# One encoder layer on one core: smaller first loads, wider attention products and a changed order of some loads

## The chip, the core and the metric

The kernel runs on one core of a Trainium2 chip. The core has a matrix engine (TensorE, PE in the profile; its weight loads are listed apart as PEld), three engines for element-wise work (VectorE or DVE, ScalarE or ACT, GpSimd or POOL), and a synchronisation engine (SyncE, SP) whose queue issues most of the transfers between HBM and the on-chip memory. Matrix products write to eight banks of an accumulator memory (PSUM). The metric is the time of one execution on the device, in microseconds (us); lower is better.

## What is computed

One layer of an encoder for two sequences of 512 tokens, width 1024, in float32: a state-space branch, a differential attention branch and a cross attention to 256 memory rows, gated and merged, then a feed-forward block. Cut to what the change touches:

```
def _diff_attention(q, k, v, lam, subln_g, lambda_init):
        s = jnp.einsum('bqhd,bkhd->bhqk', qblk, k).astype(jnp.float32) * scale
        probs = jax.nn.softmax(s, axis=-1).reshape(Bn, DIFF_HEADS, 2, Q_BLOCK, L)
        w = probs[:, :, 0] - lam * probs[:, :, 1]
        return jnp.einsum('bhqk,bkhe->bqhe', w.astype(v.dtype), v)
...
    mk, mv = jnp.split(mn @ p['w_mem_kv'][l], 2, axis=-1)
    y_x = _cross_attention(xq.reshape(Bn, L, X_HEADS, X_DH), mk, mv)
    for n in range(N_BRANCH):
        term = jax.nn.sigmoid(g[..., n * D_MODEL:(n + 1) * D_MODEL]) * (branches[n] @ p['w_up'][l, n])
        merged = term if merged is None else merged + term
    x = x + merged @ p['w_out'][l]
    xn2 = _rmsnorm(x, p['norm_ffn'][l])
    gate, up = jnp.split(xn2 @ p['w_ffn_in'][l], 2, axis=-1)
    return x + (jax.nn.silu(gate) * up) @ p['w_ffn_out'][l]
```

## The kernel before

**Products.** Every float32 operand is split into a high and a low half (`split`, L131: a copy on ScalarE that rounds, a subtraction on VectorE that keeps the rest), and each product is made as three: high by high, high by low, low by high. One product instruction takes 128 rows of weights and up to 512 columns.

**Order.** The program is written in one order, and a planner places each engine's instructions by a simulated timeline; an engine then runs its own list strictly in order. `tc.issue_after(x)` holds the instructions of its block behind `x` on the engine of `x` alone. `queued()` (L293) is such a block behind `last_w`, the last weight load so far, and so concerns SP's list. From L687 on (and again from L1166), `PE.on` keeps TensorE's list in the written order.

**The start (L304 to L322).** TensorE first multiplies zeros, `NWARM` times (L305). The loop at L311 then loads the first weight of the memory projection in two halves of 256 KB, each followed by `mem_part(i)` (L222), which loads two of the eight rows of the transposed memory in one transfer of 512 KB and splits them, scaled by a column of `vec`. `vec` itself is loaded at L118, first in SP's list. `mem_part(2)` and `mem_part(3)` follow. `mem_k(0, ...)` makes three products for each of the eight rows, in the order of the rows; `mem_k(1, ...)` follows with the second weight.

**Differential attention (L829 to L938).** There are 32 steps, one for each head `h`, sequence `s` and block `qt` of 128 queries. `scores(i)` makes the scores of two steps and their softmax; `turn(i)` transposes the 128 by 512 weights of a step on TensorE and splits them into `pH` and `pL` (tag `pT`, 4 slots); `outputs(i)` multiplies them by the values, after each second step, with 256 queries at a time; `squares` and `normed` finish a head three steps on. Between them `fill(n)` puts products from `queue`: projections, and at its end `merges()`, which multiplies branch outputs by `w_up` (`merge_units`: 24 products each). Branch outputs are loaded by `merge_load` and split by `merge_split`; `merge_in(2)` (L816) does both for the four tiles of branch 2 at one place, ahead of the third unit.

**Feed-forward, first half (L1153 to L1198).** 22 rounds of 84 products. Each round makes four sums of weights on POOL (L1040 to L1043), scales two results there (`up`, L1182) and, in rounds 4 to 18, prepares a part of the weights of the second half (`half_piece`, L1198): 128 by 128 sums on POOL (`raw_sums`, L454 to L457), a split, and a store to `wD`.

**Feed-forward, second half (L1215 to L1338).** 36 pieces of 21 products, in twelve visits (`VISITS`, of 2, 3, 3, 4, ... pieces). A piece needs two weight tiles, `wD` loads at L1255 (384 KB) and L1253 (512 KB) for the first 16 pieces; six rooms hold the weights of three pieces, so a piece's loads start when the piece three before it is done. Activations come in pairs: `pair_in` (L1211) loads two tiles of 512 KB (`fa`, `fb`, L1139 and L1140), makes sums of them and splits seven quarters. A visit starts from `y`, loaded at L1293. The last tile of activations is stored at L1318.

Of the kernel before, what the change touches and what calls it, by code (L numbers as in the profile page):

```python
# [19 lines left out]
P = 128  # L20
L = 512
# [19 lines left out]

NG = (7, 6, 3)

NWARM = 13

SCAN = (33, 40, 47, 53, 60)
ROUND = 12582912.0
# [25 lines left out]
def encoder(ctx: ExitStack, tc: tile.TileContext, a, out):  # L73
# [41 lines left out]

    ident = cst.tile([P, P], F32, name="ident")
    vec = cst.tile([P, N_VEC], F32, name="vec")
    nc.sync.dma_start(vec, a["vecs"])  # L118
# [7 lines left out]
    def vcol(name, i=0):  # L126
        o = VEC[name][0] + i
        return vec[:, o : o + 1]
# [92 lines left out]

    def mem_part(i):  # L222
        mt_ = slot("ld", [P, 2, L], name="mt")
        nc.sync.dma_start(mt_, a["memT"][:, 2 * i : 2 * i + 2, :])
        for j in range(2):
            split(mh[i][:, j, :], ml[i][:, j, :], mt_[:, j, :], scale=vcol("norm_mem", 2 * i + j))

    last_sq = None
# [79 lines left out]

    wf = wp.tile([P, DM], F32, tag="wf", name="wf")
    wh, wl = (wp.tile([P, DM], F32R, tag=n_, name=n_) for n_ in ("wh", "wl"))  # L310
    for i in range(2):  # L311
        hs = slice(i * L, (i + 1) * L)
        nc.sync.dma_start(wf[:, hs], a["w_mk"][0][:, hs])
        split(wh[:, hs], wl[:, hs], wf[:, hs])
        mem_part(i)
    mw = [(wh, wl)]
    mem_part(2)
    mem_part(3)
    mw.append(weight(a["w_mk"][1]))
    with queued():  # L320
# [412 lines left out]
    phase.close()  # L733


    open_tags(phase, v2=2, qk=12, pT=4)
    aes = ExitStack()
    ap_ = aes.enter_context(tc.tile_pool(name="att", bufs=2, reuse_waits="tile"))
    acol = aes.enter_context(tc.tile_pool(name="acol", bufs=2, reuse_waits="tile"))
# [38 lines left out]
        split(h_, l_, yt, scale=(0.125, None, 0.5)[n])  # L778
        b[0][t], b[1][t] = h_, l_

    def merge_in(n, tags="yyyy"):
        b = [None] * 4, [None] * 4
        for t in range(4):
            merge_split(b, n, t, tags[t], merge_load(n, t))
        return b

    def merge_units(n, b, m, first=False, last=False):
        gt = slot("ld", name="gl")
        nc.sync.dma_start(gt, gD[n * KD + m])
# [14 lines left out]
            split(mgh[m], mgl[m], mg[m])  # L804

    mes, zes = ExitStack(), ExitStack()
    b0, b1 = (([None] * 4, [None] * 4) for _ in range(2))
    b1_in = []

    def merges():  # L810
        res_.close()
        xp_es.close()
        open_tags(mes, side="right", mg=8, y=8)
        for m in range(KD):
            if m == 2:
                b2 = merge_in(2)  # L816
            yield from merge_units(0, b0, m, first=True)
        for m in range(KD):
            yield from merge_units(2, b2, m)
# [43 lines left out]

    def turn(i):
        h, s, qt = steps[i]
        if qt % 2 == 0:
            pT[h, s, qt // 2] = tuple(slot("pT", [P, 4, 2 * P], F32R, n_) for n_ in ("pH", "pL"))
        e0 = es.pop(i)
        tr = aux()
        for j in range(4):  # L870
            PE.transpose(tr[:, j * P : (j + 1) * P], e0[:, j * P : (j + 1) * P], ident)
        ps = slice(qt % 2 * P, qt % 2 * P + P)
        split(*(p_[:, :, ps] for p_ in pT[h, s, qt // 2]), tr.rearrange("p (j q) -> p j q", j=4))

    def outputs(i):

        h, s, qt = steps[i]
        if h == 2 and s == qt - 1 == 0:
# [11 lines left out]
        if qt == 3:  # L890
            o_ = rp.tile([P, L], F32, tag="nsq", name="osb", bufs=2)
            S.copy(o_, osb[h, s])
            osb[h, s] = o_

    def squares(i):
        h, s, _ = steps[i]
# [18 lines left out]
    for i in range(-1, n + 3):  # L915
        if i % 2 and i + 1 < n:
            scores(i + 1)
        fill(10 if i < n - 1 else 16)
        if 0 <= i < n:
            turn(i)  # L920
        if 0 < i <= n and steps[i - 1][2] % 2:
            outputs(i - 1)
        fill(10)
        if 1 < i <= n + 1 and steps[i - 2][2] == 3:
            squares(i - 2)
        if i > 2 and steps[i - 3][2] == 3:
            normed(i - 3)
        if i in (17, 19, 21, 23):
            t = (0, 1, 3, 2)[(i - 17) // 2]
            with yielding(last_e):  # L930
                merge_split(b0, 0, t, "v" if t == 3 else "qk", first[t])
        if i in (15, 17, 19, 21):
            t = (0, 1, 3, 2)[(i - 15) // 2]
            first[t] = merge_load(0, t)
# [214 lines left out]
                pass  # L1149
        return w  # L1150

    nxt_w, last_t = res0, None
    for i in range(KFF):  # L1153
        w = nxt_w or all7(i)
        nxt_w = None
        if i == 4:
            prep = prepare(pes, pieces[NPREP[0] : NPREP[1]])
            next(prep)
        elif i == KFF - 3:
            assert next(prep, None) is None  # L1160
            pes.close()
            open_tags(fes, side="right", tsa=1, tsb=1)
        if i == KFF - 1:
            with tc.issue_after(last_s[1].ins):
# [12 lines left out]
        def activate(s, gf, up):  # L1177
            nonlocal last_t
# [3 lines left out]
            PO.tensor_tensor(out=up, in0=up, in1=accs[s], op=ALU.mult)  # L1182
            V.scalar_tensor_tensor(out=ac[:, cs], in0=ac[:, cs], scalar=1.0, in1=gf, op0=ALU.add, op1=ALU.mult)
            V.tensor_tensor(out=ac[:, cs], in0=ac[:, cs], in1=up, op=ALU.mult)

        if i == KFF - 1:
            with tc.issue_after(last_sum.ins):
                activate(0, gf0, up0)
            break
        with ExitStack() as es_:  # L1190
            if i == KFF - 2:
                nxt_w = all7(i + 1)
                es_.enter_context(tc.issue_after(last_s[1].ins))
            activate(0, gf0, up0)
# [82 lines left out]
    for v, (m, lo_, hi_) in enumerate(VISITS):  # L1277
        ps = [bank() for _ in range(6)] + [aux()]
        for p in range(lo_, hi_):
            if n_p + 3 < len(pieces) and not pieces[n_p + 3][2]:  # L1280
                next(coming[n_p + 3])
            if n_p + 2 < len(pieces):
                next(coming[n_p + 2])
            for g in coming[n_p + 1 : n_p + 2]:
                for _ in g:
                    pass
            th, tl = pairs[p]
            w = made[n_p]
            n_p += 1
            if v < 4 and p == 1:  # L1290
                with queued():
                    for t in (m, m + 4):
                        nc.sync.dma_start(y[t], x1D[t])  # L1293
            for p_, (nm, o) in zip(ps, SEVEN):
                wh, wl = w[nm]
                PE.matmul(p_, wh, th[:, o], start=(p == lo_), stop=False)
                PE.matmul(p_, wh, tl[:, o], start=False, stop=False)
                PE.matmul(p_, wl, th[:, o], start=False, stop=(p == hi_ - 1))
            if v == 3 and p == 0:
                with tc.issue_after(last_sum.ins):  # L1300
                    pair_in()
            if (v, p) in ((10, 7), (10, 8), (11, 7), (11, 8)):
                keep(2)
# [11 lines left out]
            with queued(), tc.issue_after(last_sum.ins):  # L1315
                pair_in()
        if v == 2:
            nc.sync.dma_start(aD[KFF - 1], ac)  # L1318
# [520 lines left out]
```

## Time and profile before

| What | us |
|---|---|
| median of 3 runs | 1592.64 (1591.06 to 1593.86) |
| profiled execution, whole | 1595.11 |
| profiled execution, span | 1593.3 |
| PE busy in the span | 1577.1 (99%) |
| DVE, ACT, POOL busy | 1162.6, 631.0, 532.9 |
| mean granted TensorE clock | 0.996 |

The span is the time from the first to the last instruction of the program; 1.8 us of the profiled execution lie around it. The profiled execution is 2.5 us longer than the median of the runs. A row of the timeline gives the start, the duration, the engine, the line, the operation with the tiles it writes and reads, the number of merged instructions, and in brackets the idle time before it and what ended it. Products overlap, so a product's duration (0.39 us) is longer than the distance to the next one. In the view by windows each engine has its busy time and its count of instructions, followed by the granted clock (PEclk), the share of the 16 transfer engines that was busy, and GB/s.

### The profile page before, as it was taken

Reading aid. Unit: us, or ns where it says so; the run is one execution under the profiler, and the core shown is the slowest. Engines: PE = TensorE matmul, PEld = TensorE weight load, DVE = VectorE, ACT = ScalarE, POOL = GpSimd, SP = SyncE. Lnnn points to the kernel's source line nnn. Section 1 sums busy time; section 2 is a strip of 40 time slices with the busy share of each in tenths; the row PEclk is TensorE's granted clock in tenths of the full one; section 3 lists DMA queues with packets and bytes.
Section 4 is the critical chain, followed back from the end, with each engine's and each line's share of the span. In section 5 each row is a group of like instructions: output and inputs, shape, how many; then the busy total and the mean of one; then the engine's idle time right before and its main releaser. Section 6 shows DMA issues by size and latency. Waiting matters only on the chain.

```text
span 1593.3 us, 21527 instructions
## 1 busy us (share of the span) xinstructions
PE 1577.1 (99%) x7838; PEld 1317.1 (83%) x7838; DVE 1162.6 (73%) x1858; ACT 631.0 (40%) x1114; POOL 532.9 (33%) x434
## 2 busy tenths in 40 slices
PE   9999999999999999999999999999999999999997
PEld 7888888888898789878888888888888888788787
DVE  7978995077773776865545578888888878978864
ACT  6644223275652465563223343233332333223323
POOL 0010000001333320300443355766676543444663
PEclk9999999999999999999999999999999999999998
DMA  9554623576762121154543522333333323985312
GB/s 363 178 167 127 205 93 124 177 265 209 255 225 102 52 89 41 47 162 149 192 145 119 146 85 94 108 104 120 119 129 124 111 93 116 331 320 190 125 60 106
DMA packets 104890, 237.84 MB, mean 149 GB/s; under 512 B 13520, under 2 KB 45008, under 8 KB 104784
## 3 DMA queue, kind: packets, MB, share of 16 engines
q1 hardware_dynamic: 104784, 236.47, 44.0%
q8 instruction: 61, 1.00, 0.3%
q14 instruction: 45, 0.37, 0.1%
HBM read 165.16 MB, written 71.27 MB: 148 GB/s over the span
## 4 chain that ended last, share of the span: by engine, by line
PE 90%; DVE 3%; POOL 3%; DMA 2%; issue 1%; SPq 0%; ACT 0%; POOLq 0%; DVEq 0%; ACTq 0%
PE bkmm L66 78%; PE bktr L66 4%; PE bkoo L66 2%; PE bktr L69 2%; PE bksc L66 1%; PE bktr L1673 1%; DMA w<-wD 1%; DVE wl L135 1%; PE bktr L1642 1%; DMA aD<-ac 1%; PE bktr L1734 0%; PE bktr L1733 0%; PE bktr L1732 0%; PE bktr L1609 0%; DMA mt<-in_memT 0%
## 5 line engine op out<-in xcount | busy, mean ns | idle before, releaser
L66 PE MATMUL bkmm<-xh,wh 128*128 128x512 f32 x640 | 254.4, 398 | 0.0
L66 PE MATMUL bkmm<-xh,wl 128*128 128x512 f32 x640 | 250.5, 392 | 0.0
L66 PE MATMUL bkmm<-xl,wh 128*128 128x512 f32 x640 | 250.1, 391 | 0.0
L66 PE MATMUL bkmm<-th,wl 128*128 128x512 f32 (+1 forms) x621 | 240.9, 388 | 0.6 <-DVE wl L135 0.6
L66 PE MATMUL bkmm<-tl,wh 128*128 128x512 f32 (+1 forms) x621 | 241.1, 388 | 0.0
L66 PE MATMUL bkmm<-th,wh 128*128 128x512 f32 (+1 forms) x621 | 240.7, 388 | 0.0
L134 ACT CAST wh<-wf 128x1024 fp32r<-128x1024 f32 (+1 forms) x133 | 117.4, 883 | 245.2 <-PE bkmm L66 178.5
L135 DVE TENSOR_TENSOR wl<-wf,wh 128x1024 fp32r<-128x1024 f32 (+1 forms) x133 | 149.9, 1127 | 61.3 <-ACT wh L134 56.9
L66 PE MATMUL bkmm<-th,w 128*128 128x512 f32 x432 | 142.1, 395 | 3.4 <-DMA w<-wD 2.7
L66 PEld LDWEIGHTS bkmm<-xh,wh 128*128 128x128 f32 x640 | 120.3, 188 | 26.2 <-issue 3.4
L66 PEld LDWEIGHTS bkmm<-xh,wl 128*128 128x128 f32 x640 | 120.2, 188 | 26.1 <-issue 0.4
L66 PEld LDWEIGHTS bkmm<-xl,wh 128*128 128x128 f32 x640 | 120.4, 188 | 22.2
L66 PEld LDWEIGHTS bkmm<-th,wl 128*128 128x128 f32 x621 | 116.5, 188 | 25.0 <-DVE wl L135 1.1
L66 PEld LDWEIGHTS bkmm<-tl,wh 128*128 128x128 f32 x621 | 116.6, 188 | 24.0
L66 PEld LDWEIGHTS bkmm<-th,wh 128*128 128x128 f32 x621 | 116.6, 188 | 23.8
L454 POOL TENSOR_TENSOR raw<-raw 128x128 f32<-128x128 f32 x28 | 15.9, 572 | 312.4 <-DVE nb L545 230.2
L1182 POOL TENSOR_TENSOR up<-up,acc 128x512 f32<-128x512 f32 x44 | 82.4, 1891 | 80.1 <-DVE up L1120 76.4
L66 PEld LDWEIGHTS bkmm<-th,w 128*128 128x128 f32 x432 | 81.7, 189 | 24.3 <-DMA w<-wD 3.4
L800 POOL TENSOR_TENSOR mg<-mg,gl 128x1024 f32<-128x1024 f32 x16 | 43.8, 2739 | 138.3 <-DVE gl L796 133.7
L66 PE MATMUL bkmm<-tl,w 128*128 128x512 f32 x216 | 84.7, 392 | 0.0
L66 PE MATMUL bkmm<-yh,wh 128*128 128x512 f32 x192 | 76.1, 396 | 0.0
L1181 ACT ACTIVATE ac<-gf 128x512 f32<-128x512 f32 x44 | 27.8, 633 | 119.5 <-DVE gf L1180 61.0
(661 smaller groups left out, 3563.6 us busy)
## 6 DMA issues: line engine op xcount, KB each, us to landing
wf<-in_w_in SPq DMA_DIRECT2D x40, 512.0 KB, 4.0
wD<-hl SPq DMA_DIRECT2D x28, 512.0 KB, 2.9
w<-wD SPq DMA_DIRECT2D x28, 512.0 KB, 4.7
gD<-gt SPq DMA_DIRECT2D x24, 512.0 KB, 3.0
gl<-gD SPq DMA_DIRECT2D x24, 512.0 KB, 3.4
wf<-in_w_fg SPq DMA_DIRECT2D x22, 512.0 KB, 3.7
wf<-in_w_fu SPq DMA_DIRECT2D x22, 512.0 KB, 3.7
aD<-ac SPq DMA_DIRECT2D x22, 512.0 KB, 3.0
```

Source lines behind the costliest of these rows:

```text
L66: return self.put(self.eng.matmul(*args, **kw))
L69: return self.put(self.eng.transpose(*args, **kw))
L134: h = S.copy(hi, src)
L135: l_ = V.tensor_tensor(out=lo, in0=src, in1=hi.bitcast(F32), op=ALU.subtract)
L454: PO.tensor_tensor(out=a22, in0=a21, in1=a22, op=ALU.add)
L800: PO.tensor_tensor(out=mg[m], in0=mg[m], in1=gt, op=ALU.add)
L1181: last_t = S.activation(out=ac[:, cs], in_=gf, func=AF.Tanh, scale=0.5)
L1182: PO.tensor_tensor(out=up, in0=up, in1=accs[s], op=ALU.mult)
L1642: PE.matmul(kp[64 * hf : 64 * hf + 48, g * 144 : (g + 1) * 144], l48[:, ri, 4 * g4 + 2 * hf + g, :], o_[:, 4 * g4 + 2 * hf + g, :], start= ...
L1673: PE.matmul(ps[:, g * P : (g + 1) * P], w_[:, gg * P : (gg + 1) * P], u_[:, 8 * o + gg, :], start=True, stop=True)
```

## The change

The first weight comes in three parts (two of 128 KB, one of 256 KB), each row of the memory in a transfer of its own, `vec` is issued by ScalarE's queue, and ten products of zeros are made instead of thirteen. `outputs` now works once per head and sequence, on all 512 queries, and stands ahead of the transposes of the next step; `pT` has two slots of twice the size. Branch 2 is loaded and split one or two tiles at a time, over four units of `merges()`. The preparation on POOL is put behind the scaling of `up` of its round. In the second half the loads of the pairs and the store of the last activations are put behind the last weight load written so far.

```diff
-NWARM = 13
+NWARM = 10
...
-    nc.sync.dma_start(vec, a["vecs"])
+    nc.scalar.dma_start(vec, a["vecs"])
...
-        nc.sync.dma_start(mt_, a["memT"][:, 2 * i : 2 * i + 2, :])
         for j in range(2):
+            nc.sync.dma_start(mt_[:, j], a["memT"][:, 2 * i + j, :])
             split(mh[i][:, j, :], ml[i][:, j, :], mt_[:, j, :], scale=vcol("norm_mem", 2 * i + j))
...
-    for i in range(2):
-        hs = slice(i * L, (i + 1) * L)
+    for i, hs in enumerate((slice(0, 2 * P), slice(2 * P, 4 * P), slice(L, DM))):
         nc.sync.dma_start(wf[:, hs], a["w_mk"][0][:, hs])
         split(wh[:, hs], wl[:, hs], wf[:, hs])
         mem_part(i)
     mw = [(wh, wl)]
-    mem_part(2)
     mem_part(3)
...
-    open_tags(phase, v2=2, qk=12, pT=4)
+    open_tags(phase, v2=2, qk=12, pT=2)
...
         for m in range(KD):
-            if m == 2:
-                b2 = merge_in(2)
             yield from merge_units(0, b0, m, first=True)
+            for t in {4: (0,), 5: (1,), 6: (2, 3)}.get(m, ()):
+                merge_split(b2, 2, t, "y", b2_in[t])
+            for t in {3: (0,), 4: (1,), 5: (2, 3)}.get(m, ()):
+                b2_in[t] = merge_load(2, t)
...
-        if qt % 2 == 0:
-            pT[h, s, qt // 2] = tuple(slot("pT", [P, 4, 2 * P], F32R, n_) for n_ in ("pH", "pL"))
+        if qt == 0:
+            pT[h, s] = tuple(slot("pT", [P, 4, L], F32R, n_) for n_ in ("pH", "pL"))
...
-        pH, pL = pT.pop((h, s, qt // 2))
-        if qt == 1:
-            osb[h, s] = bank("oo")
-        od = osb[h, s][:, qt // 2 * 2 * P : (qt // 2 + 1) * 2 * P]
+        pH, pL = pT.pop((h, s))
+        od = bank("oo")
...
         fill(10 if i < n - 1 else 16)
+        if 0 < i <= n and steps[i - 1][2] == 3:
+            outputs(i - 1)
         if 0 <= i < n:
             turn(i)
-        if 0 < i <= n and steps[i - 1][2] % 2:
-            outputs(i - 1)
         fill(10)
...
-            PO.tensor_tensor(out=up, in0=up, in1=accs[s], op=ALU.mult)
+            last_u = PO.tensor_tensor(out=up, in0=up, in1=accs[s], op=ALU.mult)
...
-            half_piece((last_t, last_sum))
+            half_piece((last_t, last_sum, last_u))
...
             if v == 3 and p == 0:
-                with tc.issue_after(last_sum.ins):
+                with queued(), tc.issue_after(last_sum.ins):
                     pair_in()
...
         if v == 2:
-            nc.sync.dma_start(aD[KFF - 1], ac)
+            with queued():
+                nc.sync.dma_start(aD[KFF - 1], ac)
...
         if v in (3, 4, 6, 7):
-            with tc.issue_after(last_sum.ins):
+            with queued(), tc.issue_after(last_sum.ins):
                 pair_in()
```

More of the change, by code (lines that the diff above doesn't have):

```diff
@@ L779, in merge_split @@
         b[0][t], b[1][t] = h_, l_
[L781 to L785, printed above, removed]
     def merge_units(n, b, m, first=False, last=False):
@@ L806, in encoder @@
     mes, zes = ExitStack(), ExitStack()
-    b0, b1 = (([None] * 4, [None] * 4) for _ in range(2))
+    b0, b1, b2 = (([None] * 4, [None] * 4) for _ in range(3))
+    b2_in = {}
     b1_in = []
@@ L871, in turn @@
             PE.transpose(tr[:, j * P : (j + 1) * P], e0[:, j * P : (j + 1) * P], ident)
-        ps = slice(qt % 2 * P, qt % 2 * P + P)
-        split(*(p_[:, :, ps] for p_ in pT[h, s, qt // 2]), tr.rearrange("p (j q) -> p j q", j=4))
+        split(*(p_[:, :, qt * P : (qt + 1) * P] for p_ in pT[h, s]), tr.rearrange("p (j q) -> p j q", j=4))
     def outputs(i):
-        h, s, qt = steps[i]
-        if h == 2 and s == qt - 1 == 0:
+        h, s, _ = steps[i]
+        if h == 2 and s == 0:
             finish(v1_)
@@ L889, in outputs @@
             PE.matmul(od, vl[:, j, vs], pH[:, j, :], start=False, stop=(j == 3))
[L890 to L893, printed above, removed]
+        osb[h, s] = rp.tile([P, L], F32, tag="nsq", name="osb", bufs=2)
+        S.copy(osb[h, s], od)
     def squares(i):
@@ L1150, in all7 @@
         return w
-    nxt_w, last_t = res0, None
+    nxt_w, last_t, last_u = res0, None, None
     for i in range(KFF):
@@ L1177, in activate @@
         def activate(s, gf, up):
-            nonlocal last_t
+            nonlocal last_t, last_u
             cs = slice(s * L, (s + 1) * L)
```

## The prediction

> **What bounds the kernel now.** I read the busy times first, then what TensorE waited for, then the timeline around each wait.
>
> ```profile
> span 1593.3 us, 21527 instructions
> PE 1577.1 (99%) x7838; PEld 1317.1 (83%) x7838; DVE 1162.6 (73%) x1858; ACT 631.0 (40%) x1114; POOL 532.9 (33%) x434
> ...
> PE bkmm L66 <- DMA w<-wD: 2.7, 3, 2.2
> PE bktr L66 <- ACT mh L137: 1.3, 2, 0.9
> ...
> PE bktr L69 <- DVE osb L911: 0.9, 1, 0.9
> ...
> PE bkmm L66 <- DVE wl L135: 0.6, 1, 0.6
> ```
>
> The first two lines are from the page, the rest from the view of TensorE's waits (total us, times, longest). TensorE bounds the span, so time can only go where it stands still or where it makes fewer instructions. The four waits sit in four places, and each place is touched by one part of the change. I price them in order of time.
>
> **The start.** SP's list, TensorE's and ScalarE's timelines, and the views of the first weight and of the memory rows:
>
> ```profile
> 0.74 0.39 SPq L118 DMA_DIRECT2D vec<-in_vecs  x1
> 1.18 0.42 SPq L313 DMA_DIRECT2D wf<-in_w_mk  x1
> 1.65 0.42 SPq L224 DMA_DIRECT2D mt<-in_memT  x1
> 2.12 0.43 SPq L313 DMA_DIRECT2D wf<-in_w_mk  x1
> ...
> 1.18 4.90 PE L66 MATMUL bktr<-pad_r 128*128 128x128 f32 x26 [1.18 <-DVE pad_r L82]
> 6.97 0.50 PE L66 MATMUL bktr<-mh,wh 128*128 128x512 f32 x1 [0.89 <-ACT mh L137]
> ...
> 14.37 2.01 PE L66 MATMUL bktr<-mh,wh 128*128 128x512 f32 x8
> ...
> 3.95 0.62 ACT L134 CAST wh<-wf 128x512 fp32r<-128x512 f32 x1 [1.49 <-DMA wf<-in_w_mk]
> ...
> 12.52 1.05 ACT L134 CAST wh<-wf 128x1024 fp32r<-128x1024 f32 x1
> ...
> DMA to landing us min/median/max: 2.7/3.8/4.8
> ...
> L137 ACT ACTIVATE mh<-mt,vec x8: 707/709/723, 6.2 to 11.9; 128x512 fp32r<-128x512 f32 x8
> L138 DVE SCALAR_TENSOR_TENSOR ml<-mt,vec,mh x8: 743/747/752, 6.9 to 12.8; 128x512 fp32r<-128x512 f32 x8
> L224 SPq DMA_DIRECT2D mt<-in_memT x4: 423/432/459, 1.6 to 3.5; - x4
> ...
> DMA to landing us min/median/max: 4.5/6.5/7.7
> ```
>
> The landings follow from issue plus time to landing: first half of the weight 1.18 + 2.7 = 3.9, first two rows 1.65 + 4.5 = 6.1, second half 2.12 + 4.8 = 6.9, last two rows 3.5 + 7.7 = 11.2. So 256 KB took 0.8 between 6.1 and 6.9, and the 1536 KB after it 4.3, or 0.72 for each 256 KB.
>
> Without `vec` ahead of it SP issues the first weight part 1.18 - 0.74 = 0.44 earlier. That part is 128 KB smaller (0.36), so it lands at 3.9 - 0.44 - 0.36 = 3.1, and row 0 between 3.1 + 0.72 = 3.8 and, at the slow pace of the first transfers (512 KB from 3.9 to 6.1), 4.2. After the 0.71 of L137 the first product could run at 4.5 to 4.9. The zeros stand ahead of it: 26 instructions, two for each product, took 4.90, until 6.08; twenty end at 1.18 + 4.90 x 20/26 = 4.95 if all cost the same. TensorE starts between 4.95 and 6.08, I say at 5.3, instead of at 6.97.
>
> What counts is where the eighth row lets it end, because all 2560 KB still have to land: the last row at 11.2 - 0.44 = 10.8. Then 0.71 (L137), 0.75 (L138) and two products of 0.23 (below): 12.7. Before, the two rows landed together and were worked off one after the other, until 14.37, where `mem_k(1)` begins. That needs the second weight, cast from 12.52 to 13.57; 0.44 earlier is 13.1. So the second weight sets the start of `mem_k(1)`: 14.37 - 13.1 = 1.3. I take **-1.2**. The small end is 14.37 - 13.7 = 0.7, if each of the ten transfers after the first takes 0.8 (last row 3.1 + 8.0 = 11.1, second weight 1.3 behind it, then the cast); the large end is 14.37 - 12.7 = 1.7, if the cast does not bind. The five extra issues (0.42 and 0.05 each) put the second weight's issue near 6, long before its bytes can move. On ScalarE the issue of `vec` takes about 0.4 out of the 1.49 it idled before 3.95; without that cover the first cast would be 0.4 late.
>
> The Trainium skill, "DMA: Bandwidth & Descriptors", section Bandwidth, says to batch transfers to 1 MiB or more, and its fit gives each a fixed 2.0 us. Five more transfers, paid in line, would make +10 us, an estimate from that page. The trace does not agree: the second half landed 0.8 after the transfer ahead of it, so the fixed part overlaps.
>
> **Attention.** The product steps, and the wait on `osb`:
>
> ```profile
> 706.27 0.28 PE L66 MATMUL bkoo<-pL,vh 128*128 128x256 f32 x1
> ...
> 707.46 0.28 PE L66 MATMUL bkoo<-pH,vl 128*128 128x256 f32 x1
> ...
> 713.70 0.40 PE L66 MATMUL bkmm<-yh,wl 128*128 128x512 f32 x1
> 715.03 0.66 PE L69 MATMUL bktr<-ident,e 128*128 128x128 f32 x4 [0.93 <-DVE osb L911]
> ...
> 711.36 1.23 DVE L138 SCALAR_TENSOR_TENSOR yl<-yt,yh 128x1024 fp32r<-128x1024 f32 x1 [1.53 <-ACT yh L137]
> ...
> 714.23 0.74 DVE L911 SCALAR_TENSOR_TENSOR osb<-osb,g,bktr 128x512 f32<-128x512 f32 x1
> ```
>
> A product of 256 columns takes a step of (707.46 - 706.27)/10 = 0.119; one of 512 columns (1390.23 - 1385.69)/20 = 0.227, from the rows of the second half below. There are 8 x 2 x 12 = 192 of the first kind; they become 96 of the second: 22.8 - 21.8 = **-1.0**. A group's first product can take 0.11 more (0.50 at 6.97 against 0.39); for eight groups that is 0.9, so the ends are 0.1 (the new ones pay it) and 1.9 (the old ones did, for eight more).
>
> At 713.70 TensorE stood 1.33 - 0.23 = 1.1, because the splits of branch 2, put in one place, held VectorE ahead of L911. The change spreads them: **-1.1**. The last two tiles are still split together, 2 x 1.23 on VectorE, under a unit of 24 x 0.23 = 5.5; without that cover up to half of the wait returns. The memory of `pT` stays the same (four times 4 KB a partition, or twice 8).
>
> **Feed-forward, first half.** POOL, then TensorE:
>
> ```profile
> 1014.07 2.52 POOL L1182 TENSOR_TENSOR up<-up,acc 128x512 f32<-128x512 f32 x2
> ...
> 1021.44 0.39 PE L66 MATMUL bkmm<-tl,wh 128*128 128x512 f32 x1
> 1022.39 0.50 PE L66 MATMUL bkmm<-th,wl 128*128 128x512 f32 x1 [0.56 <-DVE wl L135]
> ```
>
> POOL took `up` only at 1014.07, after the first preparation sums, and so the weight sums behind it were late. With the sums behind `up` the 0.95 - 0.23 = 0.7 should go: **-0.7**. POOL is busy for 33% of the span, so the preparation finds room later in each round; if it did not, the wait would stay and the term be 0.
>
> **Feed-forward, second half.** SP's list, TensorE and the clock:
>
> ```profile
> 1380.09 0.42 SPq L1139 DMA_DIRECT2D fa<-aD  x1
> ...
> 1381.09 0.53 SPq L1318 DMA_DIRECT2D aD<-ac  x1
> 1381.72 0.40 SPq L1139 DMA_DIRECT2D fa<-aD  x1
> ...
> 1382.81 0.37 SPq L1255 DMA_DIRECT2D w<-wD  x1
> ...
> 1385.69 0.39 PE L66 MATMUL bkmm<-th,w 128*128 128x512 f32 x1
> ...
> 1390.23 0.39 PE L66 MATMUL bktr<-th,w 128*128 128x512 f32 x1
> 1392.80 0.50 PE L66 MATMUL bkmm<-th,w 128*128 128x512 f32 x1 [2.19 <-DMA w<-wD]
> ...
> 1399.87 0.39 PE L66 MATMUL bkmm<-th,w 128*128 128x512 f32 x1
> ...
> 1394.00:1398.00 4.00, 3.90 (x10) 3.14 (x11) 1.39 (x2) 0.45 (x1) 1.44 (x2) 0.57 1.03 423
> ```
>
> Two pairs (each `fa` is followed by its `fb`) and a store, five times 512 KB, stand ahead of the weights of the piece that should start at 1390.46. Its predecessor ran from 1385.69 to 1390.46, 4.77 for 21 products. The next piece began only at 1399.87, 9.4 after 1390.46: 2.3 of waiting for the first weight, then a wait for the second and a lowered clock (0.57 in the mean of that window). So 9.4 - 4.8 = **-4.6** is there to gain. The pair at 1381.72 is written where the last weight load belongs to the piece three after this one, and that load starts when this piece is done; so `queued()` moves the pair to about 1395.2. The store goes behind the load of the piece before that, to about 1390.5. That takes three times 512 KB off; at 423 GB/s it is 3.7, and the wait was 2.3, so 1.4 is the margin. If the load were late all the same, the term would be 0. The pair is then on chip at 1395.2 + 4.6 (its own 1 MB and 0.9 MB of weights at 423 GB/s) + 2.7 (the shortest landing above) = 1402.5. Its first product is due seven pieces after 1390.46, at 1423.9, so it is late for nobody if VectorE finds the time.
>
> **Sum.** -1.2 - 1.0 - 1.1 - 0.7 - 4.6 = -8.6. I keep 1.0 back for new waits, two of the size of L135's (0.6), because every list but TensorE's is planned afresh: -7.6. The profiled execution of 1595.1 would become 1587.5; the runs, 2.5 below it, 1592.6 - 7.6 = **1585.0**.
>
> **The rivals.**
>
> *The late pairs take back what the weights gain.* The pair now arrives only at 1402.5, its sums and splits meet the evacuation of the next visit on VectorE, and TensorE waits for a free bank. For it: the transfer engines were fully busy there (1.03 in the window above), and VectorE has 73% of the span. Against: 21 us of room. Without the 4.6: 1592.6 - 3.0 = 1589.6.
>
> *The clock rises later.* Six fewer zero products may leave TensorE at half clock while it waits for rows. In the window of the lowered clock above ten products began in 4.0 us where 17 fit: 7 x 0.227 = +1.6. With the gain of 1.2 at the start lost too it is 1585.0 + 2.8 = 1587.8. The Trainium skill, "TensorE: Matmul & The Clock Gate", Part 1, says the clock opens after a busy window of about 3.4 us and that the window runs freely. The trace shows the reverse step, half clock after the stop of 2.2 at 1390.
>
> *Slower: one set of `pT`.* `outputs(i-1)` now stands ahead of the transposes and needs the fourth block's `pL`. If the twenty fill products no longer cover it, TensorE stands for the copy and the subtraction at each of eight hand-overs:
>
> ```profile
> 607.24 0.69 DVE L135 TENSOR_TENSOR pL<-bktr,pH 128x512 fp32r<-128x512 f32 x1
> ...
> 608.28 0.60 PE L69 MATMUL bktr<-ident,e 128*128 128x128 f32 x4
> ```
>
> At this tight hand-over `pL` ends at 607.93, and the products, which followed these last transposes, move ahead of them to 608.28: 0.35 is left. Once that is used up, the transposes' 0.60, a copy like that at 3.95 (0.62) and the subtraction's 0.69 can lie open at each hand-over: 8 x 1.9 = +15.3, 1600.3. It decides from 7.6/8 = 0.95 for each.
>
> *The planner moves the unrelated stretches.* It re-plans the parts that had no wait. One more place like that at 1390 costs 4.6, and 1589.6 to 1592 results.
>
> **How the numbers follow.** Forecast 0.55, late pairs 0.13, clock 0.10, one set of `pT` 0.10, planner 0.12. The forecast's own range is 1581.5 (-1.7 - 1.9 - 1.1 - 0.7 - 4.6 is 1582.6; the runs scatter by 1.2 to 1.6 about their median) to 1588. For 8 in 10 I go to 1580.5 and 1592.5: the last takes in the late pairs and the planner, and leaves out the slower case. Within 0.2% means 1589.5 to 1595.8, about what a measurement of this kernel can tell from no change. Faster: 0.55 + 0.10 + half of the late pairs = 0.72. Same: the other half and most of the planner's, 0.16. Slower: 0.12.
>
> **What would show it.** The first product of `mh` starts near 5.3 and `mem_k(1)` near 13.1; 96 products of `bkoo` with 512 columns have no wait on `pL`; the waits on `osb`, on `wl` at 1021 and on `w<-wD` are gone; PEclk stays at 1.00 until the end. A wait on `pL`, on a bank (`up`, L1120) or on `fa`/`fb` would make the prediction wrong.

## The result and the profile after

The changed kernel takes 1608.97 us (median of 6 runs, 1605.30 to 1610.12), the kernel before beside it 1593.25 (6 runs, 1588.79 to 1594.49): a ratio of 1.0099, 95% interval 1.0082 to 1.0116. The forecast was 1585.0, with a range up to 1592.5. The forecast was faster; the result is slower.

The page of the changed kernel, from its profiled execution of 1609.53:

```profile
span 1607.7 us, 21318 instructions
PE 1583.2 (98%) x7736; PEld 1311.1 (82%) x7736; DVE 1173.6 (73%) x1859; ACT 628.8 (39%) x1115; POOL 538.7 (34%) x434
```

And the view of TensorE's waits (total us, times, longest):

```profile
PE bkmm L66 <- DVE wl L135: 9.9, 12, 1.9
PE bkmm L66 <- DVE mg L788: 1.6, 1, 1.6
...
PE bkmm L66 <- ACT p L1116: 1.1, 1, 1.1
```

Both waits that the change aimed at in the second half and in attention (`w<-wD` 2.7, `osb` 0.9) are gone from the list. In their place stands a wait on `wl`, twelve times, 9.9 us. Eleven of the twelve, 9.4 us, lie between 1119 and 1288, in the rounds of feed-forward that prepare the second half; the twelfth, 0.5, lies at 369. The shift of markers along the two profiles (start of the same product, after minus before) says where the time went:

| Stretch | shift gained in it, us |
|---|---|
| start, up to the fourth copy of `mf` | -0.5 |
| from there to the end of cross attention | +1.4 |
| attention and merge | +0.5 |
| feed-forward, first half | +16.3 |
| second half, pieces 6 and 7 | -4.65 |
| second half, the rest | +1.4 |
| whole | +14.4 |

So one stretch holds the result. One window of it, before (first row) and after (second); the columns are busy times with instruction counts, then granted clock, DMA share, GB/s:

```profile
1040.00:1300.00 260.00, 260.00 (x1149) 215.29 (x1148) 222.61 (x246) 81.32 (x108) 162.87 (x115) 1.00 0.34 116
```

```profile
1040.00:1300.00 260.00, 250.43 (x1073) 202.13 (x1073) 213.95 (x228) 73.75 (x101) 160.24 (x120) 0.99 0.32 110
```

TensorE began 76 products fewer in the same 260 us; at 260/1149 = 0.226 each that is 17.2 us (the stretch as a whole lost 0.9 less, since the wait at 1021 did go). Idle time is 260.00 - 250.43 = 9.6 of it. POOL is as busy as before: the loss is one of order, not of load.

One round of the changed kernel shows how. First POOL, then VectorE, then TensorE (start, duration, in brackets the idle time before and what ended it):

```profile
1112.03 2.20 POOL L1172 TENSOR_TENSOR up<-up,acc 128x512 f32<-128x512 f32 x1 [8.36 <-DVE up L1110]
1114.19 0.91 POOL L452 TENSOR_TENSOR raw<-raw 128x128 f32<-128x128 f32 x1
1115.17 0.46 POOL L453 TENSOR_TENSOR raw<-raw 128x128 f32<-128x128 f32 x1
1115.59 1.29 POOL L1172 TENSOR_TENSOR up<-up,acc 128x512 f32<-128x512 f32 x1
...
1116.92 0.94 DVE L1174 TENSOR_TENSOR ac<-ac,up 128x512 f32<-128x512 f32 x1 [2.14 <-POOL up L1172]
1117.78 0.68 DVE L1110 TENSOR_TENSOR gf<-bkmm,p 128x512 f32<-128x512 f32 x1
1118.38 1.21 DVE L135 TENSOR_TENSOR wl<-ws,wh 128x1024 fp32r<-128x1024 f32 x1
1119.51 1.77 DVE L1170 TENSOR_TENSOR gf<-gf,acc 128x512 f32<-128x512 f32 x1
...
1118.48 0.39 PE L66 MATMUL bkmm<-tl,wh 128*128 128x512 f32 x1
1119.64 0.50 PE L66 MATMUL bkmm<-th,wl 128*128 128x512 f32 x1 [0.78 <-DVE wl L135]
```

The same place in the kernel before:

```profile
1103.44 0.46 POOL L454 TENSOR_TENSOR raw<-raw 128x128 f32<-128x128 f32 x1 [2.62 <-DMA raw<-in_w_fo]
...
1105.39 0.46 POOL L457 TENSOR_TENSOR raw<-raw 128x128 f32<-128x128 f32 x1
1106.32 3.91 POOL L1182 TENSOR_TENSOR up<-up,acc 128x512 f32<-128x512 f32 x2 [0.47 <-DVE up L1120]
...
1110.27 0.69 DVE L1184 TENSOR_TENSOR ac<-ac,up 128x512 f32<-128x512 f32 x1 [1.19 <-POOL up L1182]
1110.88 0.69 DVE L1120 TENSOR_TENSOR gf<-bkmm,p 128x512 f32<-128x512 f32 x1
1111.60 0.69 DVE L1180 TENSOR_TENSOR gf<-gf,acc 128x512 f32<-128x512 f32 x1
1112.20 1.22 DVE L135 TENSOR_TENSOR wl<-ws,wh 128x1024 fp32r<-128x1024 f32 x1
```

Before, POOL did its two scalings of `up` back to back. Now two of the four preparation sums stand between them (0.91 + 0.46 = 1.4). VectorE's product with `up` waits for the second scaling: 2.14 where it had waited 1.19. It is so in twelve rounds, with 2.13 to 2.15 in each, where the kernel before has 1.18 or 1.19. VectorE works off its list in order, so an evacuation and the subtraction that makes the next `wl` come late too, and TensorE stops for `wl`. POOL had been idle for 8.36 just before; in the kernel before the sums stood in that gap. The planner answered the edge on two more lists: on VectorE the subtraction of `wl` now stands ahead of the scaling of `gf` by `acc` (it stood behind it), and ScalarE's list changed with it.

In some rounds the price is higher. The timeline of such a place, VectorE, POOL, TensorE:

```profile
1139.29 2.33 DVE L135 TENSOR_TENSOR wl<-ws,wh 128x1024 fp32r<-128x1024 f32 x1
...
1139.27 1.27 POOL L1030 TENSOR_TENSOR ws<-wf 128x512 f32<-128x512 f32 x1 [0.18 <-DMA wf<-in_w_fu]
...
1141.67 0.70 PE L66 MATMUL bkmm<-th,wl 128*128 128x512 f32 x1 [1.88 <-DVE wl L135]
1142.17 0.63 PE L66 MATMUL bkmm<-th,wh 128*128 128x512 f32 x1
...
1145.15 0.43 PE L66 MATMUL bkmm<-tl,wh 128*128 128x512 f32 x1
```

And a window of it (the 0.72 is the granted clock):

```profile
1143.00:1147.00 4.00, 4.00 (x14) 3.19 (x13) 3.30 (x4) 2.09 (x3) 3.06 (x2) 0.72 0.00 0
```

The subtraction took 2.33 instead of 1.21; a sum on POOL had begun 0.02 before it. Four of the 25 subtractions of this kind between 1040 and 1300 took 2.28 to 2.33, and ahead of each such a sum had begun, by less than 0.1. Where VectorE was first (1118.38 in the round above, POOL at 1118.40), its subtraction took 1.21 and POOL's sum 2.33. The longer stop, 1.88, was followed by a lowered clock: eight products began 0.427 apart, which costs 8 x 0.2 = 1.6. That happened twice (the other stop, 1.84, is at 1204). The Trainium skill, "GPSIMD Engine Reference", section 1, says that GpSimd shares its interface to the on-chip memory with VectorE and that instructions of VectorE with two inputs from there contend for it. The trace agrees, with 2.33 for whichever of the two came second, against 1.21 and 1.27 for the first.

Of the 17.2, 9.6 are idle time, 2 x 1.6 the lowered clock, and 11 x 0.27 = 3.0 the edges of the stops (behind 1118.48 the next product starts 1.16 later, 0.94 more than a step, of which 0.78 is shown as idle; and a product behind a stop takes a step of 0.34 instead of 0.23). That is 15.8; the other 1.4 isn't accounted for.

### The profile page after: what moved, and what is told of

It reads as the page before. It is cut to its first block, busy times and chain, and to the rows that moved or that the text cites. A ratio compares the mean times of both kernels' runs of the same rounds, so it can differ in the third digit from the quotient of the medians.

```text
span 1607.7 us, 21318 instructions
## 1 busy us (share of the span) xinstructions
PE 1583.2 (98%) x7736; PEld 1311.1 (82%) x7736; DVE 1173.6 (73%) x1859; ACT 628.8 (39%) x1115; POOL 538.7 (34%) x434
## 4 chain that ended last, share of the span: by engine, by line
PE 75%; DVE 7%; POOL 6%; DMA 5%; issue 5%; ACT 2%; SPq 0%; POOLq 0%; DVEq 0%; ACTq 0%
PE bkmm L66 64%; PE bktr L66 3%; PE bkoo L66 2%; POOL up L1172 2%; PE bktr L69 2%; DMA aD<-ac 1%; PE bksc L66 1%; DVE wl L135 1%; PE bktr L1664 1%; DVE gf L1170 1%; DMA yt<-bD 1%; DVE hl L138 1%; DMA wf<-in_w_fu 1%; DVE ac L1173 1%; DVE ac L1174 1%
## 5 line engine op out<-in xcount | busy, mean ns | idle before, releaser
L135 DVE TENSOR_TENSOR wl<-wf,wh 128x1024 fp32r<-128x1024 f32 (+2 forms) x134 | 152.3, 1137 | 60.6 <-ACT wh L134 55.8
L134 ACT CAST wh<-wf 128x1024 fp32r<-128x1024 f32 (+2 forms) x134 | 117.3, 876 | 182.9 <-PE bkmm L66 157.7
L1172 POOL TENSOR_TENSOR up<-up,acc 128x512 f32<-128x512 f32 x44 | 78.7, 1798 | 143.8 <-DVE up L1110 140.1
```

The lines of the kernel that those rows point to most:

```text
L134: h = S.copy(hi, src)
L135: l_ = V.tensor_tensor(out=lo, in0=src, in1=hi.bitcast(F32), op=ALU.subtract)
L1172: last_u = PO.tensor_tensor(out=up, in0=up, in1=accs[s], op=ALU.mult)
```

## The experiments

Theory A: the edge (`last_u`) is the cause, and everything else together is a small gain. Rival B: every list is planned afresh, and the loss comes from that. In what follows 0.0010 in a ratio is 1.6 us, and each ratio is against the runs of the kernel before in the same batch.

### The edge taken out, and the edge alone

```diff
 # e1_no_edge, against the changed kernel
-            half_piece((last_t, last_sum, last_u))
+            half_piece((last_t, last_sum))
 # e2_edge_alone, against the kernel before
+            last_u = PO.tensor_tensor(out=up, in0=up, in1=accs[s], op=ALU.mult)
...
-            half_piece((last_t, last_sum))
+            half_piece((last_t, last_sum, last_u))
```

> The changed kernel with the edge of the preparation taken out again (the sums of `raw` are held behind the tanh and the last sum only, as before); all other edits stay. Theory A, the edge: it cost the first half of feed-forward 16.3 us (the piece that opens the second half moved by 17.7, the first round's end by 1.4), so this run should come to 1609.0 - 16.3 = 1592.7, within 2 us, and the waits on `wl` should fall from 9.9 us to about 0.6. Rival B, the afresh planned lists of the other edits: the waits on `wl` stay and the time stays near 1609.

Measured: 1592.72, ratio 0.9989 (0.9980 to 0.9998), and no wait on `wl` in the list: theory A's number. The two medians, from different batches, differ by 1608.97 - 1592.72 = 16.3 us; the first half of feed-forward takes 422.04 in the profile, 438.84 with the edge. All the rest together gains 0.11%.

> The kernel before with nothing but the edge behind `up`. Theory A: 1593.3 + 16.3 = 1609.6, within 2 us, with some ten waits on `wl` between 1110 and 1290. Rival B: within 2 us of 1593.3, because the edge needs the other edits to hurt.

Measured: 1605.21, ratio 1.0072 (1.0058 to 1.0085). Rival B falls: the edge alone makes the kernel slower by 11. But it is 4.4 short of theory A's number. Its row in the view of waits:

```profile
PE bkmm L66 <- DVE wl L135: 8.8, 14, 0.8
```

And the group of its subtractions of this kind between 1040 and 1300 (minimum, median, maximum in ns, first and last start):

```profile
L135 DVE TENSOR_TENSOR wl<-ws,wh x25: 1207/1215/1219, 1047.8 to 1294.0; 128x1024 fp32r<-128x1024 f32 x25
```

Here no subtraction was stretched, no stop in this window was longer than 0.8, and no stretch of products ran at the lowered clock. The first half takes 435.23, 12.7 more than the 422.57 of before; the whole shows less because pieces 6 and 7 of the second half took 11.25 in this execution and 14.17 in the one of before (more on this below). So the order by itself costs 12.7 in the first half, and the changed kernel has 3.6 more there. Its two stretches at the lowered clock are 2 x 1.6 of that; there is only one profile of it, and which of two instructions begins first, by less than 0.1, may change from execution to execution.

The loss is not the wait for the second scaling alone. One round on VectorE, from one `ac<-ac,gf` to that of the next round, takes 20.93 here (1108.11 to 1129.04) and took 18.88 before (1103.64 to 1122.52). Of these 2.05, the longer wait for `up` is 0.94. A wait of 0.70 for ScalarE's tanh at 1120.62 is new: the tanh needs `gf<-gf,acc`, which now stands behind the subtraction of `wl`.

### The sums behind both scalings

```diff
-            last_u = PO.tensor_tensor(out=up, in0=up, in1=accs[s], op=ALU.mult)
+            last_u.append(PO.tensor_tensor(out=up, in0=up, in1=accs[s], op=ALU.mult))
...
-            half_piece((last_t, last_sum, last_u))
+            half_piece((last_t, last_sum, *last_u[-2:]))
```

> The changed kernel with the sums of `raw` behind both scalings of `up` of the round instead of behind the one that is written last. In the changed kernel two of the four sums stand between the two scalings on POOL; the product `ac<-ac,up` stands on VectorE behind the later scaling, with an evacuation and the split of `wl` behind it. Theory A1: these 1.4 us between the scalings are what hurts; then the waits on `wl` nearly go and the time falls to 1592 to 1595. Theory A2: what hurts is that all four sums (2.6 us) stand ahead of the next sums of weights; then the waits on `wl` stay and the time is within 3 us of 1609.

Measured: 1592.32, ratio 0.9988 (0.9979 to 0.9997); no wait on `wl`. POOL in the same round:

```profile
1106.69 3.90 POOL L1172 TENSOR_TENSOR up<-up,acc 128x512 f32<-128x512 f32 x2 [5.41 <-DVE up L1110]
1110.56 0.46 POOL L452 TENSOR_TENSOR raw<-raw 128x128 f32<-128x128 f32 x1
...
1112.50 0.79 POOL L455 TENSOR_TENSOR raw<-raw 128x128 f32<-128x128 f32 x1
1113.25 2.27 POOL L1030 TENSOR_TENSOR ws<-wf 128x512 f32<-128x512 f32 x1
```

All four sums stand behind both scalings and ahead of the sums of weights, and that is free: theory A2 falls. VectorE's and ScalarE's lists are those of the run without the edge again, so this run takes back the two sums between the scalings and the exchange on VectorE together; what each costs by itself, no run shows.

It also shows what `last_u` was. With an edge to both scalings the sums moved behind both; with an edge to the one that the program writes last they stood behind the first on POOL. That fits only if POOL runs the scaling that is written last first: "behind `last_u`" left the other one behind the sums. The kernel's text agrees: `quadrants` makes `c22`, the input of the scaling that is written last (`up1`), one line ahead of `c21`, that of the other.

> The kernel before with the preparation's sums behind both scalings of `up`, and nothing else. Theory A1 (the place between the two scalings was the whole price): the wait on `wl` at 1021 goes, none of the later ones comes, and the prediction's term of -0.7 holds: 1593.5 against 1594.3, a ratio of 0.9990 to 1.0002. Rival A2 (the edge behind `up` costs by itself, and other edits of the changed kernel made room for it): waits on `wl` as with the edge alone, near 1605.

```diff
 # against the kernel before, the edit of the run above
+            last_u.append(PO.tensor_tensor(out=up, in0=up, in1=accs[s], op=ALU.mult))
...
+            half_piece((last_t, last_sum, *last_u[-2:]))
```

Measured: 1593.45, ratio 0.9995 (0.9985 to 1.0004), no wait on `wl` at 1021 or later. The first half takes 421.69 from its first product to the first product of the second half, 422.57 before: -0.9, the size of the prediction's term. But the first half isn't the same in every execution: the eight profiles without the edge lie between 421.99 and 422.76, the four with both scalings between 421.69 and 421.71, so the gain is 0.3 to 1.1. The time itself can't show so little.

### The other edits one by one

```diff
 # e3_loads_alone
             if v == 3 and p == 0:
-                with tc.issue_after(last_sum.ins):
+                with queued(), tc.issue_after(last_sum.ins):
...
         if v == 2:
-            nc.sync.dma_start(aD[KFF - 1], ac)
+            with queued():
+                nc.sync.dma_start(aD[KFF - 1], ac)
...
         if v in (3, 4, 6, 7):
-            with tc.issue_after(last_sum.ins):
+            with queued(), tc.issue_after(last_sum.ins):
```

> The kernel before with nothing but the later loads of the pairs and the later store in the second half of feed-forward. The prediction's term says -4.6 (1588.7) and no wait on `w<-wD`. In the changed kernel the same piece won 4.65 (its shift went from +17.85 to +13.20), while places after it lost 1.1 to 2.0 again; if these losses come with the later loads, this run is only -3 (1590.2).

Measured: 1591.87, ratio 0.9989 (0.9980 to 0.9998), -1.8 us: less than either number, and the interval (0.3 to 3.2 gained) leaves out the whole 4.6. Pieces 6 and 7 took 9.52 instead of 14.17: the 4.65 is there. Pieces 24 to 31 took 41.04 instead of 40.03.

> The kernel before with the start alone: first weight in three parts, one row of memory in each transfer, `vec` from ScalarE, ten products of zeros. The prediction's term is -1.2 (0.7 to 1.7), measured where `mem_k(1)` begins. The profiles of the changed kernel show the first copy of `mf` 0.7 earlier and everything after the fourth copy 0.5 earlier, so the rival is -0.5, too little for a verdict. The same code started 2.4 later in another execution (a run with before's own start had its first copy of `mf` at 16.98 instead of 14.57), so a single profile cannot tell; the medians decide.

Its diff is the one of the start in the change above. Measured: 1593.58, ratio 0.9995 (0.9987 to 1.0004). Not to be told from nothing. The first copy of `mf` begins at 13.99.

> The kernel before with the wide products of attention alone (`outputs` once per head and sequence, ahead of the transposes; two slots of `pT`). The prediction's term is -1.0 (1592.2 to 1593.2). In the changed kernel this edit and the spread of branch 2 together lost 1.6 between the end of cross attention and the end of attention, where -2.1 had been predicted. If the loss comes from this edit (hand-overs without cover), the run is 1 to 2 us slower than before and the shift is spread over eight places.

Its diff is the one of `turn`, `outputs` and `pT` above. Measured: 1593.15, ratio 0.9993 (0.9985 to 1.0002). From the last product of cross attention to the last of attention it took 256.63, where the profiles without any edit of attention have 257.03 to 258.57 (seven, median 257.28): the loss in attention doesn't come from here. The two later runs with the wide products and without the spread of branch 2 have 256.61 and 256.89, so all three lie below all seven.

> The kernel before with the spread of branch 2's loads and splits alone. The prediction's term is -1.1: the wait on `osb` goes. The rival: the splits now stand ahead of the products with the gates on VectorE (`mg`), so TensorE waits for a bank there instead (1.6 us at L788 in the changed kernel), and the run is 0.5 to 1.5 slower than before.

Its diff is the one of `merges()` above. Measured: 1596.08, ratio 1.0008 (0.9999 to 1.0016): +1.3, with an interval that just reaches no change, against a term of -1.1. Its stretch of attention is 258.25, which lies within the seven unedited ones, so alone it proves no loss. With the wide products in, it does: 257.72 to 258.88 in the three profiles that have both edits, against the 256.61 to 256.89 of the three without this one. VectorE and TensorE of the changed kernel at the place:

```profile
713.21 1.22 DVE L138 SCALAR_TENSOR_TENSOR yl<-yt,yh 128x1024 fp32r<-128x1024 f32 x1 [2.41 <-ACT yh L137]
714.36 0.68 DVE L541 TENSOR_REDUCE nb<-bktr 128x1 f32<-128x512 f32 x1
714.96 1.87 DVE L541 TENSOR_REDUCE nb<-bksc 128x1 f32<-128x512 f32 x3
...
718.46 0.68 DVE L788 SCALAR_TENSOR_TENSOR mg<-gl,bkmm 128x512 f32<-128x512 f32 x1
...
719.19 0.50 PE L66 MATMUL bkmm<-yh,wh 128*128 128x512 f32 x1 [1.62 <-DVE mg L788]
```

The split of branch 2 still stands in VectorE's list where it must wait (2.41) for ScalarE's half, and the softmax of a step and the evacuation with the gate (`mg`) are queued behind it. TensorE now waits for that bank instead of for `osb`.

### One execution or every execution

> The kernel before, unchanged, profiled once more. In the run with the wide products alone every engine's list from feed-forward on is the one of before, and yet its pieces 6 to 8 took 10.95 where before took 14.18 (two pieces without a wait take 9.54). Theory V: the wait on `w<-wD` and the lowered clock at piece 7 differ from execution to execution; then pieces 6 to 8 of this run may take anything from 10 to 15, and the prediction's term of -4.6 was the size of one execution. Rival F: it is fixed by the lists and the run with the wide products escaped for another reason; then they take 14.2 again, within 0.5.

Nothing is edited. Its profile took 13.95 for pieces 6 and 7. TensorE's row behind the wait, here and in the run with the wide products alone, whose lists from feed-forward on are those of before:

```profile
1392.65 0.50 PE L66 MATMUL bkmm<-th,w 128*128 128x512 f32 x1 [1.90 <-DMA w<-wD]
```

```profile
1390.26 0.50 PE L66 MATMUL bkmm<-th,w 128*128 128x512 f32 x1 [0.58 <-DMA w<-wD]
```

The seven profiles without the later loads give 14.17, 13.95, 13.95, 13.46, 13.43, 11.25 and 10.95; the seven with them give 9.52 every time. So theory V holds in part: the loss is there in each, 3.9 to 4.65 in five and 1.4 to 1.7 in two, though the lists of that stretch are the same. The five are those whose granted clock fell behind the wait; the two waited for 0.58 and 0.81 and kept their clock. Why the wait was shorter there isn't known. The term of -4.6 was the largest of the seven.

### What adds up

> The kernel before with the two edits that won time in the profiles, the start and the later loads of the second half, and none of the others. -0.5 to -1.2 from the start and -2.4 from the loads (4.65 won at one piece, some 2 lost again around other pieces in the run with the loads alone): 2.9 to 3.6 below before, a ratio of 0.9977 to 0.9982, and below the changed kernel without its edge by about 1.6, the loss in attention. The rival, that the losses are anywhere the lists are planned afresh: no better than that kernel (0.9989).

Measured: 1592.48, ratio 0.9986 (0.9977 to 0.9995). Its profile is 2.97 shorter, as expected; the runs are 2.2 shorter (the interval reaches from 0.8 to 3.7) and can't be told from the kernel without its edge, where 1.6 between the two had been expected.

> The changed kernel with both scalings ahead of the sums and without the spread of branch 2's loads and splits. By the medians so far the start is worth -0.7, the wide products -1.1, the later loads -1.8 to -2.4, the sums behind both scalings 0 to -0.7: together 3.6 to 4.9, so 1589.4 to 1590.7 where before is at 1594.3 (0.9969 to 0.9977). Rival: the gains are taken from the same places and do not add; then it is no better than 0.9986, the best so far.

It is the changed kernel with both scalings ahead of the sums and `merges()` as before. Measured: 1590.55, ratio 0.9978 (0.9969 to 0.9987), just outside the expected ratio. The gains seem to add, but the interval still reaches the rival's 0.9986.

> As the run without branch 2's spread, but the pairs loaded after visits 6 and 7 are not held behind the last weight load. In the profiles with the later loads the pieces from the 24th to the 32nd lose 1.0 to 1.5, where the copy of a bank (`p`) stands on ScalarE behind a split that waits for POOL's sums of late raw weights; in SP's list the held pairs and `fl` stand ahead of these raw loads. If that is the reason, the wait on `p` of 1.0 to 1.4 goes and the run is 1.0 to 1.5 faster than the run beside it. Rival: the wait stays, because VectorE and ScalarE are full there anyway.

```diff
-            with queued(), tc.issue_after(last_sum.ins):
+            with ExitStack() as q_:
+                if v in (3, 4):
+                    q_.enter_context(queued())
+                q_.enter_context(tc.issue_after(last_sum.ins))
                 pair_in()
```

Measured: 1589.44, ratio 0.9969 (0.9960 to 0.9979). TensorE's waits in the late visits, first without this edit, then with it:

```profile
PE bkmm L66 <- ACT p L1119: 1.3, 1, 1.3
PE bkmm L66 <- DVE nsq L1113: 0.2, 1, 0.2
```

```profile
PE bkmm L66 <- DVE u L1113: 0.6, 1, 0.6
PE bkmm L66 <- ACT w L137: 0.3, 1, 0.3
```

The wait on `p` is gone, and more than half of it is given back as a wait on `u` and one on `w`. Pieces 24 to 31 take 40.79 instead of 41.35, where before has 40.03: 0.6 of the 1.3 comes back at the place. The gain of 1.1 in the medians is within the expected 1.0 to 1.5, but the two intervals overlap, and what goes beyond 0.6 is not located. In ScalarE's list of the run without the edit the copy of `p` stood behind a split that waited for late raw weights:

```profile
1490.75 0.63 ACT L137 ACTIVATE w<-acc 128x512 fp32r<-128x512 f32 x1 [2.54 <-POOL acc L455]
1491.29 0.57 ACT L1119 COPY p<-bkmm 128x512 f32<-128x512 f32 x1
```

This is the best version: 0.31% or 4.9 us below the kernel before.

## Why the prediction was wrong

**The step that failed** is the first half of feed-forward: "With the sums behind `up` the 0.95 - 0.23 = 0.7 should go", with the bound "if it did not, the wait would stay and the term be 0". Measured there: +16.3 in the changed kernel, +12.7 with the edge alone. Two things were wrong in it. It read "behind `up`" as behind the scaling of the round, but a round has two scalings, the edge named one, and that one runs first; the other was pushed behind two sums (this follows from the runs with both scalings). And it gave the edge no price on the bad side: it argued from POOL's 33% that there is room, where the question was who stands behind the delayed scaling. The row for that was in the profile of before: VectorE idles 1.19 for `up` at 1110.27 in each such round, with an evacuation and the subtraction of `wl` queued behind it. A delay there is passed on at once. The place that the term was read from was the exception: at 1016.62 VectorE had waited 4.52 for `up`. The edge took this one wait to 1.18 and raised twelve others from 1.18 or 1.19 to 2.13 to 2.15. With the edge to both scalings the same term measures -0.3 to -1.1.

**Start, -1.2:** the first product came at 5.32, as forecast (5.3). The working then let the second weight set the start of `mem_k(1)`, at 13.1. ScalarE's and TensorE's rows of the changed kernel:

```profile
12.66 1.05 ACT L134 CAST wh<-wf 128x1024 fp32r<-128x1024 f32 x1 [0.51 <-DMA wf<-in_w_mk]
...
13.76 0.96 PE L66 MATMUL bktr<-mh,wh 128*128 128x512 f32 x3
```

It does set it, right behind the end of that cast, but the weight's bytes came no earlier: the cast begins at 12.66, and had begun at 12.52. So `mem_k(1)` begins 14.37 - 13.76 = 0.6 earlier. Over all profiles, seven with the new start and seven with the old one, the cast begins at 12.88 against 12.52 (medians), `mem_k(1)` at 13.98 against 14.37, the first copy of `mf` at 13.99 against 14.57 and the fourth at 31.24 against 31.53. The limit was named rightly, but the 0.44 by which the second weight should come earlier were not there; 0.3 to 0.6 of the 1.2 were. The small end, 0.7, does not come out of its own terms either: 11.1 + 1.3 + 1.05 is 13.45, not 13.7, and leaves 0.9.

**Wide products, -1.0:** right, as far as can be told. -0.65 in the stretch, -1.1 by the runs (from 2.4 less to 0.3 more); no wait on `pL`, and the rival of one set of `pT` didn't come about.

**Branch 2, -1.1:** not there. +1.3 alone (-0.2 to +2.6), and the stretch of attention says a loss too where the wide products are in. In the changed kernel the wait on `osb` went and a wait on `mg` came; alone, 0.5 on `osb` stayed beside 1.2 on `mg`. The prediction named the last two tiles' splits as the risk; by the rows above, the place that hurt was one split whose input from ScalarE came late. The wait on `osb` itself isn't fixed either: it was between 0.7 and 2.2 in profiles whose attention is the one of before.

**Second half, -4.6:** right at its place (4.65), and too large for the whole. Pieces 24 to 31 gave 1.0 to 1.5 back, about half of it because the pairs held back at visits 6 and 7 pushed later loads; and the loss that it removes varies between executions. The run of the loads alone gained 1.8 (0.3 to 3.2). The rival of late pairs had the right idea at another place and engine.

**The clock's rival** had no part. In the seven profiles with ten zero products the clock first opens at 5.2 to 6.9, in the seven with thirteen at 4.7 to 6.8, and the only one that loses it again in the start (11.8 to 15.2, in the run with the later loads alone) has thirteen.

**The planner's rival**, that stretches which no edit touches would move, had no part: with the wide products alone, or with the edge alone, SP's list from feed-forward on is the one of before. What the planner did move stands beside the edits, as on VectorE in the rounds with the edge. By the runs the parts without the edge are -0.8 - 1.1 + 1.3 - 1.8 = -2.4; together they measure -1.8 (0.9989), which the intervals can't tell apart.

The 1.4 between the start and the end of cross attention appear in the profile of the changed kernel alone, and not in that of the kernel without the edge, whose lists are the same on every engine up to 1002. Why they came in that execution stays open.

## What to carry to other kernels

An edge "behind the last of them" has to name the one that runs last, not the one that is written last; where the order is planned, give an edge to each. Before an instruction is delayed on an engine that has time to spare, look for who waits for the instruction next to it: a short wait of an in-order engine that is already there in every round (here 1.19 on VectorE) passes any delay on to all that is queued behind it. A wait measured in one profiled execution is the size of that execution; a second profile of the same kernel says what of it is always there.

## What the runs showed of the hardware

A subtraction of 128 by 1024 on VectorE took 1.21 or 2.33, depending on whether it or a sum on POOL began first, by as little as 0.02.

A sum of 128 by 512 on POOL (`ws`) took 2.33 where it came second (at 1118.40 in the changed kernel) and 1.27 where it came first (at 1139.27).

In feed-forward a lowered clock followed every stop of 1.77 to 2.48 (seven in all profiles; 1.88 above, 2.19 in the kernel before). In attention none followed a stop of 1.62 (at 719.19 above), nor one of 2.23 in the run with the start alone. That run's rows:

```profile
716.36 0.66 PE L69 MATMUL bktr<-ident,e 128*128 128x128 f32 x4 [2.23 <-DVE osb L909]
716.77 0.48 PE L66 MATMUL bkmm<-yh,wh 128*128 128x512 f32 x1
```

And its window, at a granted clock of 1.00:

```profile
714.00:719.00 5.00, 2.77 (x15) 2.28 (x15) 4.96 (x9) 3.26 (x8) 0.00 (x0) 1.00 0.66 203
```

What tells them apart is in the traces' record of the granted clock, from which PEclk is taken. From where the clock first opens, every change of it lies a whole number of steps of 3.413 later: it falls after 1389.22, 407 steps, in the kernel before and after 1136.64, 333 steps, in the changed kernel, and a lowered stretch lasts one step, 3.41. Laid on these steps, TensorE stood idle for 1.67 to 2.48 in eight of them, over all fourteen profiles, and each of the eight is followed by a step at half the clock (seven in feed-forward, one in the start). No step with 1.56 or less is. The 1.88 above lies in one step; the 2.23 is divided between two, with no more than 1.56 of idle time in either. The time from 1575 on is left out: there the clock falls with as little as 0.7 of idle time in a step, so idle time is not the whole rule.

The Trainium skill, "TensorE: Matmul & The Clock Gate", Part 1, says that the clock falls after an idle window of about 3.4 us that runs freely. The trace agrees on the window, 3.413, and that it runs on regardless of the stops; it differs in how much of it must be idle, since 1.67 was enough.
